# Four feed-forwards of a decoder trunk, each with its own layout of the split weights and direction of the moving rows

## The chip, the cores and the metric

One Trainium2 chip; the program runs on one of its cores. The metric is the device time in microseconds of one execution. PE is the matrix engine (TensorE), with its weight loads shown as PEld; DVE is VectorE, ACT is ScalarE, POOL is GpSimd and SP the engine that issues most transfers.

## The reference, cut to what matters

Two layers, each a half-step feed-forward, a token mixing and a second half-step feed-forward, over 512 tokens of width 1024; the hidden width of a feed-forward is 2816.

```python
def _swiglu(h, wg, wu, wd):
    return (jax.nn.silu(h @ wg) * (h @ wu)) @ wd
...
    for i in range(DEPTH):
        h = _rmsnorm(x, ffn1_norm[i])
        x = x + 0.5 * _swiglu(h, ffn1_w_gate[i], ffn1_w_up[i], ffn1_w_down[i])
        h = _rmsnorm(x, mix_norm[i])
        x = x + _mixing(h, positions, w_in[i], w_out[i], fox_forget_bias[i], lbs[i],
                        hgrn_out_norm[i])
        h = _rmsnorm(x, ffn2_norm[i])
        x = x + 0.5 * _swiglu(h, ffn2_w_gate[i], ffn2_w_up[i], ffn2_w_down[i])
    return _rmsnorm(x, final_norm)
```

The mixing (three token mixers between an input and an output projection) is changed only in where its tiles lie.

## The kernel before, in words

The stream x is kept transposed in on-chip memory: eight tiles x0 to x7 of 128 rows (width) by 512 columns (tokens), in the pool `keep`. Each matrix product with weights is made from float32 values split in two parts of the shorter type float32r: a high part (the value rounded) and a low part (what the rounding left). `split_block` (L182, L184) splits the normalised stream into xh and xl, eight tiles each, also in `keep`. `load_split` (L240 to L245) loads a chunk of weights from memory by a transfer on SP into `raw` (three buffers), writes the high part `wh` by a cast on ACT (L243) and the low part `wl` by a subtraction on DVE (L245), each into a tile of its own with two buffers in the pool `wp`. The two are placed ahead of other work in the order that the scheduler makes (`tc.high_priority(AHEAD)`).

`mm3` (L250 to L252) then issues three matmuls for one slice of 128 by 128 weights: high weights with high rows, high weights with low rows, low weights with high rows. The weights are the stationary operand, loaded before each matmul; the 512 columns of rows are the moving operand, and a PSUM tile of 128 by 512 collects the sum.

`ffn` runs two stages. Gate and up: for each of 22 blocks of the hidden width, a chunk of eight slices of gate weights and one of up weights, 24 matmuls each, into PSUM tiles `gu_ps` (four buffers shared under the name acc). DVE and ACT make silu(gate) x up and split it into hh and hl (L377 to L385), 22 tiles of each in the pool `ffn`. Down: for each of the eight blocks of x, chunks of 8, 7 and 7 slices, 66 matmuls into `d_ps`, then DVE adds half of it to x (L394) and `after` splits and squares the new block (L182 to L194). So a feed-forward has 22 x 2 x 24 = 1056 matmuls of gate and up and 8 x 66 = 528 of down, all of one shape. The kernel has four: the first and the second one of each of two layers. The row norm is summed from squares (`square_block`, L190 to L194, tile sq with two buffers), finished in `norm_finish` (L213 to L231) and applied late, as the row vector rb (two buffers), to the PSUM results. The output projection of the mixing is a shorter run of the same `mm3`, four blocks at a time, which end six matmuls apart.

Where tiles lie follows from the order of the pools and the sizes of their tiles: const (with a spacer `pad` of PAD = 48 words), keep, wp, small, and then ffn or mix in turn. The helper `lines` rounds small tiles up to 64 bytes. All tiles of keep and wp are multiples of 512 bytes, so xh, xl, wh and wl begin at one offset modulo 512 bytes; the tiles of small, between wp and ffn, add up to 128 bytes less than a multiple of 512.

Of the kernel before, what the change touches and what calls it, by code (L numbers as in the profile page):

```python
# [10 lines left out]
F32 = mybir.dt.float32  # L11
# [14 lines left out]
LEVELS = (1, 2, 4, 8, 16, 32, 64)  # L26
AHEAD = 400
CHAIN = 100
PAD = 48


def shape_constants():
# [95 lines left out]
def hybrid_trunk(ctx: ExitStack, tc: tile.TileContext, a, out):  # L128
    nc = tc.nc
    V, S, G, PE = nc.vector, nc.scalar, nc.gpsimd, nc.tensor  # L130

    const = ctx.enter_context(tc.tile_pool(name="const", bufs=1))
    keep = ctx.enter_context(tc.tile_pool(name="keep", bufs=1))
    wp = ctx.enter_context(tc.tile_pool(name="wp", bufs=2))
    small = ctx.enter_context(tc.tile_pool(name="small", bufs=2))
    acc_p = ctx.enter_context(tc.tile_pool(name="acc", bufs=4, space=bass.MemoryType.PSUM))
    gen_p = ctx.enter_context(tc.tile_pool(name="gen", bufs=1, space=bass.MemoryType.PSUM))

# [12 lines left out]
        return gen_p.tile([128, 512], F32, tag=tag, name=name)  # L151


    const.tile([128, PAD], F32, name="pad")
    x = [keep.tile([128, T], F32, name=f"x{k}") for k in range(KB)]
    par = const.tile([128, 64], F32, name="par")
    raws = []
# [17 lines left out]
    def norm_block(k, g, nrm):  # L175

        split_block(k, g)
        square_block(k, nrm)
# [8 lines left out]
    def square_block(k, nrm):  # L187
        if k == 0:
            nrm["ss"] = small.tile([128, T], F32, tag="ss", name="ss", bufs=1)
            S.activation(nrm["ss"], x[k], AF.Square)  # L190
        else:
            sq = small.tile([128, T], F32, tag="sq", name="sq")
            S.activation(sq, x[k], AF.Square)
            V.tensor_tensor(out=nrm["ss"], in0=nrm["ss"], in1=sq, op=ALU.add)  # L194

# [23 lines left out]

    def norm_finish(nrm, copy=True):  # L220
        r = norm_rows(nrm)
        dg = small.tile([128, NB, 128], F32, tag="sq", name="dg")
        for b in range(NB):
            V.tensor_scalar(out=dg[:, b, :], in0=ident, scalar1=r[:, b:b + 1], scalar2=None,
                            op0=ALU.mult)
        ps = gen("pt", "rb_ps")
        PE.matmul(ps, ones, dg.rearrange("p b t -> p (b t)"), start=True, stop=True)
        if not copy:
            return r, ps
        rb = small.tile([128, T], F32, tag="rb", name="rb", bufs=2)  # L230
        S.copy(rb, ps)  # L231
        return r, rb

    def load_split(src, n, cols):

        if raws:
            raw = raws.pop(0)
        else:
            raw = wp.tile([128, n, cols], F32, tag="raw", name="raw", bufs=3)
            nc.sync.dma_start(out=raw, in_=src)  # L240
        with tc.high_priority(AHEAD):
            wh = wp.tile([128, n, cols], R32, tag="wh", name="wh")
            S.copy(wh, raw)  # L243
            wl = wp.tile([128, n, cols], R32, tag="wl", name="wl")
            V.tensor_tensor(out=wl, in0=raw, in1=wh.bitcast(F32), op=ALU.subtract)  # L245
        return wh, wl

    def mm3(ps, lh, ll, rh, rl, first, last):

        PE.matmul(ps, lh, rh, start=first, stop=False)  # L250
        PE.matmul(ps, lh, rl, start=False, stop=False)  # L251
        PE.matmul(ps, ll, rh, start=False, stop=last)  # L252
# [4 lines left out]
    def gvec(key, k):  # L257
        return par[:, gcol[key] + k:gcol[key] + k + 1]
# [101 lines left out]
        lower_bounds()  # L360


    def ffn(l, wg, wu, wd, after, rb, early=None):
        with tc.tile_pool(name="ffn", bufs=1, reuse_waits="tile") as fp:
            hh, hl = [], []
            for j in range(FB):
                if j == 4 and early:
                    early()
                part = []
                for w in (wg, wu):  # L370
                    wh, wl = load_split(w[l, j], KB, 128)
                    ps = acc("gu_ps")
                    for k in range(KB):
                        mm3(ps, wh[:, k, :], wl[:, k, :], xh[k], xl[k], k == 0, k == KB - 1)
                    part.append(ps)
                g = fp.tile([128, T], F32, tag="g", name="g", bufs=2)
                V.tensor_tensor(out=g, in0=part[0], in1=rb, op=ALU.mult)  # L377
                S.activation(g, g, AF.Silu)
                u = fp.tile([128, T], F32, tag="u", name="u", bufs=2)
                V.tensor_tensor(out=u, in0=part[1], in1=rb, op=ALU.mult)  # L380
                V.tensor_tensor(out=u, in0=u, in1=g, op=ALU.mult)  # L381
                h1 = fp.tile([128, T], R32, name=f"hh{j}")
                S.copy(h1, u)  # L383
                h2 = fp.tile([128, T], R32, name=f"hl{j}")
                V.tensor_tensor(out=h2, in0=u, in1=h1.bitcast(F32), op=ALU.subtract)  # L385
                hh.append(h1)
                hl.append(h2)
            for d in range(KB):
                ps = acc("d_ps")
                for j0, j1 in ((0, 8), (8, 15), (15, 22)):  # L390
                    wh, wl = load_split(wd[l, d, :, j0:j1, :], j1 - j0, 128)
                    for j in range(j0, j1):
                        mm3(ps, wh[:, j - j0, :], wl[:, j - j0, :], hh[j], hl[j], j == 0, j == FB - 1)
                V.scalar_tensor_tensor(out=x[d], in0=ps, scalar=0.5, in1=x[d], op0=ALU.mult, op1=ALU.add)  # L394
                after(d)


    def mixing(l, after, r, rb):
# [38 lines left out]
        otl = {kind: [pair(f"ol{kind}", f"ol{kind}", R32)] for kind in "fd"}  # L437
        amat, obl = {}, {}
        at = [lines(mp, [128, 8], tag=f"ad{p}", name=f"ad{p}") for p in range(2)]

        def put_out(kind, b, o, n):

# [215 lines left out]
            return hv  # L658

        ho = [slot(f"ho{b}", (128, 4, 128), f"ho{b}") for b in range(NB)]  # L660
        hss = [lines(mp, [128, NB, 2], tag=f"hss{p}", name=f"hss{p}") for p in range(2)]
        hrs = [None, None]

        def states(p, hv):
            am, ob = amat[p], obl[p]
            for b in range(NB):
                po = gen("lv", "ho_ps")
                for hh in range(2):
                    cross = {
                        (0, 1): ob[:, 2, hh * 256:hh * 256 + 128],  # L670
                        (2, 3): ob[:, 2, hh * 256 + 128:hh * 256 + 256],
                        (0, 2): ob[:, hh, 0:128], (0, 3): ob[:, hh, 128:256],
                        (1, 2): ob[:, hh, 256:384], (1, 3): ob[:, hh, 384:512],
                    }
                    h = 2 * p + hh
                    hs = slice(h * 128, (h + 1) * 128)
                    ps = po[:, hh * 128:(hh + 1) * 128]
                    for j in range(b + 1):
                        lhs = cross[j, b] if j < b else am[:, hh, b * 128:(b + 1) * 128]
                        PE.matmul(ps, lhs, hv[j // 2][:, j % 2, hs], start=j == 0, stop=j == b)  # L680
                    V.scalar_tensor_tensor(out=ho[b][:, h, :], in0=hv[b // 2][:, b % 2, hs],
                                           scalar=at[p][:, hh * NB + b:hh * NB + b + 1], in1=ps,
                                           op0=ALU.mult, op1=ALU.add)
                    sq = mp.tile([128, 128], F32, tag="hsq", name="hsq", bufs=1)
                    S.activation(sq, ho[b][:, h, :], AF.Square, accum_out=hss[p][:, b, hh:hh + 1])
                yield
            ss = hss[p]
            V.tensor_scalar(out=ss, in0=ss, scalar1=1.0 / 128, scalar2=EPS, op0=ALU.mult, op1=ALU.add)
            hrs[p] = rsqrt(ss.rearrange("p b h -> p (b h)"), [128, 8], f"hr{p}")
# [51 lines left out]
    for l in range(L):  # L741
# [8 lines left out]
        nrm = {}  # L750
        if l + 1 < L:
            ffn(l, a["ffn2_w_gate"], a["ffn2_w_up"], a["ffn2_w_down"],
                lambda d: norm_block(d, gvec(("ffn1_norm", l + 1), d), nrm), rb)
            r, rb = norm_finish(nrm)
        else:
            def last(d):
                square_block(d, nrm)
                if d == KB - 2:
                    warm = lines(small, [128, 1], tag="warm", name="warm")
                    S.activation(warm, nrm["ss"][:, 0:1], AF.Sqrt)  # L760

            ffn(l, a["ffn2_w_gate"], a["ffn2_w_up"], a["ffn2_w_down"], last, rb)
            _, rb = norm_finish(nrm, copy=False)
            for d in range(KB):
                V.scalar_tensor_tensor(out=x[d], in0=x[d], scalar=gvec("final", d), in1=rb,
                                       op0=ALU.mult, op1=ALU.mult)
                (nc.scalar if d % 2 else nc.sync).dma_start(out=out[d * 128:(d + 1) * 128, :], in_=x[d])
# [17 lines left out]
```

## Time and profile before

| | |
|---|---|
| median of 3 runs | 2109.16 us (2108.77 to 2109.34) |
| the profiled execution's own time | 2108.85 us |
| its span, first to last instruction | 2107.1 us |
| PE busy | 2080.3 us, 99% of the span |
| DVE, ACT busy | 993.5 us (47%), 691.6 us (33%) |
| mean granted TensorE clock | 0.997 of full speed |

Matmuls are pipelined: a record of a 512-column matmul is some 390 ns long and overlaps the next one, so what a matmul costs is the distance from its start to the next start, and the busy share of PE alone does not tell it.

### The profile page before, as it was taken

How to read it: one execution, taken by the hardware profiler on the slowest of the kernel's cores; microseconds unless marked ns; L12 is line 12 of the kernel's file. 1: busy time of each engine (PE TensorE's matmuls, PEld its weight loads, DVE VectorE, ACT ScalarE, POOL GpSimd, SP SyncE). 2: the span in 40 equal slices, each digit the busy share in tenths (PEclk: the TensorE clock that was granted, in tenths of full speed). 3: DMA queues.
4: the chain of work that ended last, by engine and by line, in shares of the span. 5: the costliest groups of instructions: out<-in, count | busy, mean ns of one | idle time of the engine just before them, and what ended most of it. 6: DMA issues, size and time to landing. Idle time of an engine off the chain costs nothing.

```text
span 2107.1 us, 23700 instructions
## 1 busy us (share of the span) xinstructions
PE 2080.3 (99%) x9622; PEld 1688.9 (80%) x9622; DVE 993.5 (47%) x1590; ACT 691.6 (33%) x1005; POOL 13.0 (1%) x18
## 2 busy tenths in 40 slices
PE   8999999999999999999999999999999999999997
PEld 6888888888777888888888888888887778888885
DVE  7444433556364544443344443336554554444323
ACT  5323222333353423222233322232344443323221
POOL 0000000000000000000000000000000000000000
PEclk9999999999999999999999999999999999999998
DMA  5322333211122222233332223332211122222332
GB/s 166 100 91 99 95 93 94 94 60 51 50 69 67 97 92 99 100 94 92 95 98 93 100 96 91 99 100 70 65 57 51 56 85 90 100 98 92 95 96 69
DMA packets 54373, 184.35 MB, mean 87 GB/s; under 512 B 6888, under 2 KB 7016, under 8 KB 54264
## 3 DMA queue, kind: packets, MB, share of 16 engines
q1 hardware_dynamic: 53656, 181.73, 27.1%
q8 instruction: 75, 1.23, 0.2%
q10 hardware_dynamic: 576, 1.05, 0.1%
q14 instruction: 34, 0.28, 0.0%
q0 software_dynamic: 32, 0.07, 0.0%
HBM read 180.69 MB, written 2.10 MB: 87 GB/s over the span
## 4 chain that ended last, share of the span: by engine, by line
PE 97%; DVE 2%; ACT 1%; DMA 0%; issue 0%; SPq 0%; DVEq 0%
PE gu_ps L252 15%; PE gu_ps L251 15%; PE gu_ps L250 15%; PE d_ps L252 8%; PE d_ps L250 8%; PE d_ps L251 8%; PE lv_ps L501 2%; PE sc_ps L552 2%; PE po L571 2%; PE o_ps L250 1%; PE o_ps L251 1%; PE o_ps L252 1%; PE ho_ps L680 1%; PE pt_ps L564 1%; PE v_ps L425 1%; PE v_ps L426 1%
## 5 line engine op out<-in xcount | busy, mean ns | idle before, releaser
L243 ACT CAST wh<-raw 128x1024 fp32r<-128x1024 f32 (+2 forms) x350 | 357.6, 1022 | 1112.7 <-issue 417.4
L245 DVE TENSOR_TENSOR wl<-raw,wh 128x1024 fp32r<-128x1024 f32 (+2 forms) x350 | 415.5, 1187 | 321.5 <-ACT wh L243 319.4
L250 PE MATMUL gu_ps<-xh,wh 128*128 128x512 f32 x1408 | 548.8, 390 | 7.5 <-ACT wh L243 7.5
L252 PE MATMUL gu_ps<-xh,wl 128*128 128x512 f32 x1408 | 550.4, 391 | 0.0
L251 PE MATMUL gu_ps<-xl,wh 128*128 128x512 f32 x1408 | 548.3, 390 | 0.0
L250 PEld LDWEIGHTS gu_ps<-xh,wh 128*128 128x128 f32 x1408 | 264.9, 188 | 63.6 <-ACT wh L243 7.5
L252 PEld LDWEIGHTS gu_ps<-xh,wl 128*128 128x128 f32 x1408 | 264.8, 188 | 56.1 <-issue 1.0
L251 PEld LDWEIGHTS gu_ps<-xl,wh 128*128 128x128 f32 x1408 | 264.8, 188 | 55.4 <-DVE xl L184 0.2
L252 PE MATMUL d_ps<-hh,wl 128*128 128x512 f32 x704 | 278.1, 395 | 0.0
L250 PE MATMUL d_ps<-hh,wh 128*128 128x512 f32 x704 | 278.1, 395 | 0.0
L251 PE MATMUL d_ps<-hl,wh 128*128 128x512 f32 x704 | 278.1, 395 | 0.0
L380 DVE TENSOR_TENSOR u<-gu_ps,rb 128x512 f32<-128x512 f32 x88 | 60.8, 691 | 269.2 <-PE gu_ps L252 269.0
L252 PEld LDWEIGHTS d_ps<-hh,wl 128*128 128x128 f32 x704 | 132.1, 188 | 32.2
L251 PEld LDWEIGHTS d_ps<-hl,wh 128*128 128x128 f32 x704 | 132.1, 188 | 32.1
L250 PEld LDWEIGHTS d_ps<-hh,wh 128*128 128x128 f32 x704 | 132.1, 188 | 32.1
L377 DVE TENSOR_TENSOR g<-gu_ps,rb 128x512 f32<-128x512 f32 x88 | 60.8, 691 | 178.7 <-PE gu_ps L252 176.6
L383 ACT CAST hh<-u 128x512 fp32r<-128x512 f32 x88 | 54.8, 623 | 61.2 <-DVE u L381 61.2
L394 DVE SCALAR_TENSOR_TENSOR x<-d_ps,x 128x512 f32<-128x512 f32 x32 | 22.1, 692 | 95.3 <-PE d_ps L252 95.3
L381 DVE TENSOR_TENSOR u<-u,g 128x512 f32<-128x512 f32 x88 | 60.9, 692 | 8.4
L501 PEld LDWEIGHTS lv_ps<-hQ,hk 128*128 128x128 f32 x448 | 55.8, 191 | 8.7 <-issue 5.9
L385 DVE TENSOR_TENSOR hl<-u,hh 128x512 fp32r<-128x512 f32 x88 | 60.3, 686 | 4.1 <-ACT hh L383 4.1
L571 PEld LDWEIGHTS po<-vv,pt 128*128 128x128 f32 x320 | 42.2, 190 | 19.7 <-DVE pt L569 7.8
(236 smaller groups left out, 2104.8 us busy)
## 6 DMA issues: line engine op xcount, KB each, us to landing
raw<-in_ffn_w_gate SPq DMA_DIRECT2D x88, 512.0 KB, 3.5
raw<-in_ffn_w_up SPq DMA_DIRECT2D x88, 512.0 KB, 3.5
raw<-in_w_in SPq DMA_DIRECT2D x58, 512.0 KB, 3.5
raw<-in_ffn_w_down SPq DMA_DIRECT2D x64, 448.0 KB, 3.3
raw<-in_ffn_w_down SPq DMA_DIRECT2D x32, 512.0 KB, 3.5
raw<-in_w_out_dh SPq DMA_DIRECT2D x16, 384.0 KB, 2.9
x<-in_x SPq DMA_DIRECT2D x8, 256.0 KB, 6.3
raw<-in_w_out_f SPq DMA_DIRECT2D x4, 512.0 KB, 3.6
```

What stands on the lines that cost most here:

```text
L243: S.copy(wh, raw)
L245: V.tensor_tensor(out=wl, in0=raw, in1=wh.bitcast(F32), op=ALU.subtract)
L250: PE.matmul(ps, lh, rh, start=first, stop=False)
L251: PE.matmul(ps, lh, rl, start=False, stop=False)
L252: PE.matmul(ps, ll, rh, start=False, stop=last)
L377: V.tensor_tensor(out=g, in0=part[0], in1=rb, op=ALU.mult)
L380: V.tensor_tensor(out=u, in0=part[1], in1=rb, op=ALU.mult)
L381: V.tensor_tensor(out=u, in0=u, in1=g, op=ALU.mult)
L383: S.copy(h1, u)
L385: V.tensor_tensor(out=h2, in0=u, in1=h1.bitcast(F32), op=ALU.subtract)
L501: PE.matmul(ps[:, e:e + 64], K[:, hh, s], Q[:, hh, s].rearrange("p (n two c) -> p n two c", two=2, c=c)[:, :, 1, :], start=True, stop=True)
L571: PE.matmul(po[:, h * HD:(h + 1) * HD], pt[:, j * 128:(j + 1) * 128], val[:, j, h * HD:(h + 1) * HD], start=j == 0, stop=j == b)
```

## The change

Each feed-forward gets a layout for the two parts of its weights and a direction for its moving rows. High and low part now share one tile `ww`. In layer 0 (mode "apart") each slice's 128 high words and 128 low words follow one another, each with a gap of 16 words. In layer 1 (mode "mixed") high and low words alternate, so that each part lies at every second word, with 16 words of gap after a slice's 256. The mixing keeps all high slices ahead of all low ones. In the second feed-forward of each layer (`turned`) the moving rows are read, and the PSUM columns written, from the last to the first. The pools are put in another order with other spacers; sq, rb and dg have one buffer; two small tiles of the mixing move.

```diff
-PAD = 48
+PAD = 96
...
-    const = ctx.enter_context(tc.tile_pool(name="const", bufs=1))
+    align = ctx.enter_context(tc.tile_pool(name="align", bufs=1))
     keep = ctx.enter_context(tc.tile_pool(name="keep", bufs=1))
     wp = ctx.enter_context(tc.tile_pool(name="wp", bufs=2))
+    const = ctx.enter_context(tc.tile_pool(name="const", bufs=1))
     small = ctx.enter_context(tc.tile_pool(name="small", bufs=2))
+    fill = ctx.enter_context(tc.tile_pool(name="fill", bufs=1))
...
-    const.tile([128, PAD], F32, name="pad")
+    align.tile([128, 32], F32, name="pad0")
+    fill.tile([128, PAD], F32, name="pad1")
...
-            sq = small.tile([128, T], F32, tag="sq", name="sq")
+            sq = small.tile([128, T], F32, tag="sq", name="sq", bufs=1)
...
-        dg = small.tile([128, NB, 128], F32, tag="sq", name="dg")
+        dg = small.tile([128, NB, 128], F32, tag="sq", name="dg", bufs=1)
...
-        rb = small.tile([128, T], F32, tag="rb", name="rb", bufs=2)
+        rb = small.tile([128, T], F32, tag="rb", name="rb", bufs=1)
...
-    def load_split(src, n, cols):
+    def load_split(src, n, cols, mode=None):
...
-            wh = wp.tile([128, n, cols], R32, tag="wh", name="wh")
+            ww = wp.tile([128, n * (2 * cols + (32 if mode == "apart" else 16 if mode else 0))], R32, tag="ww", name="ww")
+            if mode == "mixed":
+                ww = ww.rearrange("p (n c) -> p n c", n=n)[:, :, 0:2 * cols].rearrange("p n (c two) -> p n two c", two=2)
+            elif mode == "apart":
+                ww = ww.rearrange("p (n two c) -> p n two c", n=n, two=2)[:, :, :, 0:cols]
+            else:
+                ww = ww.rearrange("p (two n c) -> p n two c", n=n, two=2)
+            wh, wl = ww[:, :, 0, :], ww[:, :, 1, :]
             S.copy(wh, raw)
-            wl = wp.tile([128, n, cols], R32, tag="wl", name="wl")
             V.tensor_tensor(out=wl, in0=raw, in1=wh.bitcast(F32), op=ALU.subtract)
         return wh, wl
 
-    def mm3(ps, lh, ll, rh, rl, first, last):
-
+    def mm3(ps, lh, ll, rh, rl, first, last, turned=False):
+
+        if turned:
+            ps, rh, rl = ps[:, ::-1], rh[:, ::-1], rl[:, ::-1]
...
-    def ffn(l, wg, wu, wd, after, rb, early=None):
+    def ffn(l, wg, wu, wd, after, rb, early=None, turned=False):
+        mode = "mixed" if l else "apart"
...
-                    wh, wl = load_split(w[l, j], KB, 128)
+                    wh, wl = load_split(w[l, j], KB, 128, mode)
...
-                    wh, wl = load_split(wd[l, d, :, j0:j1, :], j1 - j0, 128)
+                    wh, wl = load_split(wd[l, d, :, j0:j1, :], j1 - j0, 128, mode)
...
-                    sq = mp.tile([128, 128], F32, tag="hsq", name="hsq", bufs=1)
+                    sq = small.tile([128, 128], F32, tag="sq", name="hsq", bufs=1)
...
-            ffn(l, a["ffn2_w_gate"], a["ffn2_w_up"], a["ffn2_w_down"], last, rb)
+            ffn(l, a["ffn2_w_gate"], a["ffn2_w_up"], a["ffn2_w_down"], last, rb, turned=True)
```

## Rows read from the trace of the kernel before

**Rows 1.** The page's head and its part 1, busy time by engine.
```profile
span 2107.1 us, 23700 instructions
...
PE 2080.3 (99%) x9622; PEld 1688.9 (80%) x9622; DVE 993.5 (47%) x1590; ACT 691.6 (33%) x1005; POOL 13.0 (1%) x18
```

**Rows 2.** The chain of waits that ended last, its shares by line.
```profile
PE gu_ps L252 15%; PE gu_ps L251 15%; PE gu_ps L250 15%; PE d_ps L252 8%; PE d_ps L250 8%; PE d_ps L251 8%; PE lv_ps L501 2%; PE sc_ps L552 2%; PE po L571 2%; PE o_ps L250 1%; PE o_ps L251 1%; PE o_ps L252 1%; PE ho_ps L680 1%; PE pt_ps L564 1%; PE v_ps L425 1%; PE v_ps L426 1%
```

**Rows 3.** Costliest groups: shape, count, busy us, mean ns, idle before, its releaser.
```profile
L243 ACT CAST wh<-raw 128x1024 fp32r<-128x1024 f32 (+2 forms) x350 | 357.6, 1022 | 1112.7 <-issue 417.4
L245 DVE TENSOR_TENSOR wl<-raw,wh 128x1024 fp32r<-128x1024 f32 (+2 forms) x350 | 415.5, 1187 | 321.5 <-ACT wh L243 319.4
L250 PE MATMUL gu_ps<-xh,wh 128*128 128x512 f32 x1408 | 548.8, 390 | 7.5 <-ACT wh L243 7.5
...
L252 PEld LDWEIGHTS gu_ps<-xh,wl 128*128 128x128 f32 x1408 | 264.8, 188 | 56.1 <-issue 1.0
...
L252 PE MATMUL d_ps<-hh,wl 128*128 128x512 f32 x704 | 278.1, 395 | 0.0
```

**Rows 4.** Windows: stretch, us, busy us (count) of each engine, PEclk, DMA.
```profile
30.00:250.00 220.00, 220.00 (x972) 182.21 (x972) 114.05 (x195) 71.49 (x91) 0.00 (x0) 1.00 0.30 96
252.00:374.00 122.00, 122.00 (x525) 98.14 (x524) 42.29 (x47) 32.58 (x39) 0.95 (x1) 1.00 0.32 93
```

**Rows 5.** Timeline of PE: start us, length us, instruction; the ends of down.
```profile
251.72 0.40 PE L250 MATMUL d_ps<-hh,wh 128*128 128x512 f32 x1
...
374.69 0.39 PE L252 MATMUL d_ps<-hh,wl 128*128 128x512 f32 x1
```

**Rows 6.** Timeline of PE inside gate and up, and inside down.
```profile
80.36 0.39 PE L250 MATMUL gu_ps<-xh,wh 128*128 128x512 f32 x1
80.59 0.39 PE L251 MATMUL gu_ps<-xl,wh 128*128 128x512 f32 x1
...
300.02 0.39 PE L250 MATMUL d_ps<-hh,wh 128*128 128x512 f32 x1
300.25 0.40 PE L251 MATMUL d_ps<-hl,wh 128*128 128x512 f32 x1
300.49 0.39 PE L252 MATMUL d_ps<-hh,wl 128*128 128x512 f32 x1
300.71 0.40 PE L250 MATMUL d_ps<-hh,wh 128*128 128x512 f32 x1
```

**Rows 7.** Timeline of PE after a break, an FK product of the mixing.
```profile
611.86 0.40 PE L250 MATMUL fk_ps<-xh,wh 128*128 128x512 f32 x1
612.10 0.39 PE L251 MATMUL fk_ps<-xl,wh 128*128 128x512 f32 x1
612.32 0.39 PE L252 MATMUL fk_ps<-xh,wl 128*128 128x512 f32 x1
...
613.71 0.39 PE L252 MATMUL fk_ps<-xh,wl 128*128 128x512 f32 x1
613.94 0.39 PE L250 MATMUL fk_ps<-xh,wh 128*128 128x512 f32 x1
```

**Rows 8.** Timeline of PE at the kernel's start; four matmuls lie between these two.
```profile
9.81 0.63 PE L251 MATMUL gu_ps<-xl,wh 128*128 128x512 f32 x1
...
11.94 0.63 PE L250 MATMUL gu_ps<-xh,wh 128*128 128x512 f32 x1
```

**Rows 9.** The chain in order of time, one level of the decay product.
```profile
434.95 1.73 PE lv_ps L501 x16
```

**Rows 10.** Groups of DVE and ACT, the whole span.
```profile
L510 DVE TENSOR_TENSOR hQ<-hQ,hf 128x512 f32<-128x512 f32 x28 | 19.4, 692 | 0.0
...
L194 DVE TENSOR_TENSOR ss<-ss,sq 128x512 f32<-128x512 f32 x49 | 33.7, 687 | 1.1 <-ACT sq L193 0.7
L193 ACT ACTIVATE sq<-x 128x512 f32<-128x512 f32 x49 | 30.1, 619 | 10.7 <-DVE x L394 9.8 <-DVE ss L194 0.8
```

**Rows 11.** Waits: who waited for whom, us in all, times, longest us.
```profile
ACT wh L243 <- PE d_ps L251: 273.7, 72, 4.1
```

More of the change, by code (lines that the diff above doesn't have):

```diff
@@ L370, in ffn @@
                 for w in (wg, wu):
-                    wh, wl = load_split(w[l, j], KB, 128)
+                    wh, wl = load_split(w[l, j], KB, 128, mode)
                     ps = acc("gu_ps")
                     for k in range(KB):
-                        mm3(ps, wh[:, k, :], wl[:, k, :], xh[k], xl[k], k == 0, k == KB - 1)
+                        mm3(ps, wh[:, k, :], wl[:, k, :], xh[k], xl[k], k == 0, k == KB - 1, turned)
                     part.append(ps)
@@ L390, in ffn @@
                 for j0, j1 in ((0, 8), (8, 15), (15, 22)):
-                    wh, wl = load_split(wd[l, d, :, j0:j1, :], j1 - j0, 128)
+                    wh, wl = load_split(wd[l, d, :, j0:j1, :], j1 - j0, 128, mode)
                     for j in range(j0, j1):
-                        mm3(ps, wh[:, j - j0, :], wl[:, j - j0, :], hh[j], hl[j], j == 0, j == FB - 1)
+                        mm3(ps, wh[:, j - j0, :], wl[:, j - j0, :], hh[j], hl[j], j == 0, j == FB - 1, turned)
                 V.scalar_tensor_tensor(out=x[d], in0=ps, scalar=0.5, in1=x[d], op0=ALU.mult, op1=ALU.add)
@@ L439, in mixing @@
         at = [lines(mp, [128, 8], tag=f"ad{p}", name=f"ad{p}") for p in range(2)]
+        hss = [lines(mp, [128, NB, 2], tag=f"hss{p}", name=f"hss{p}") for p in range(2)]
         def put_out(kind, b, o, n):
@@ L660, in mixing @@
         ho = [slot(f"ho{b}", (128, 4, 128), f"ho{b}") for b in range(NB)]
-        hss = [lines(mp, [128, NB, 2], tag=f"hss{p}", name=f"hss{p}") for p in range(2)]
         hrs = [None, None]
@@ L752, in hybrid_trunk @@
             ffn(l, a["ffn2_w_gate"], a["ffn2_w_up"], a["ffn2_w_down"],
-                lambda d: norm_block(d, gvec(("ffn1_norm", l + 1), d), nrm), rb)
+                lambda d: norm_block(d, gvec(("ffn1_norm", l + 1), d), nrm), rb, turned=True)
             r, rb = norm_finish(nrm)
```

## The prediction

> **What bounds the kernel.** I read the page from the top. The span is 2107.1 us and PE is busy in 99% of it; DVE at 47% and ACT at 33% are not near [rows 1]. The profiled execution took 2108.85 us, so 1.75 us lie around the span, and the median of the runs, 2109.16, is 0.3 us above it; I sum against 2108.9 and give the result against the median. The chain of waits is PE for 97%; the three product lines of the feed-forwards make 3 x 15% (gate and up) and 3 x 8% (down), 69% of the span, some 1454 us [rows 2]. So the time is the number of feed-forward matmuls times the distance between their starts. The numbers are 4224 (gate and up) and 2112 (down) in the groups [rows 3]: for each of the four feed-forwards 1056 and 528. The change keeps every one of them; only the distance can move.
>
> The distance comes from the windows [rows 4]. 972 matmuls in 220 us; a record is 390 ns long, so about 1.7 of them hang over the edges: 220/970.3 = **226.7 ns** for gate and up. 122/(525 - 1.7) = 233.1 for down; there the first and the last matmul of a stage start at 251.72 and 374.69, 527 distances, **233.3 ns** [rows 5], which I use. The granted clock is 1.00 in all. [...]
>
> [...] In the timeline gate/up ticks evenly, 0.22 to 0.23, while down changes between 0.22 and 0.24 from one matmul to the next [rows 6]; operation, shape and clock are the same. What differs is where the operands lie: by the sizes of the tiles in the code, weights and xh/xl start at the same offset modulo 512 bytes, while hh/hl start 128 bytes off. After a break, in one FK product of the mixing, which reads xh like gate/up, the first distances are uneven (0.24, 0.22, 0.23), and ten matmuls later it is back at 0.23 [rows 7]: something locks in. [...] The load has time: 188 ns a record, and about 40 ns of idle before each [rows 3].
>
> [...]
>
> **The change, part by part.**
> Apart (layer 0): slices of high and low part stand next to each other, each with 64 bytes of gap, so the place relative to the moving row changes with every k. Ends: it keeps the locked 226.7, or runs unlocked as in down, 233.3. I take the middle, 230: 1056 x 3.3 = +3.5 us for each of the two feed-forwards; down is unlocked already and stays. Together **+7.0**.
> Mixed (layer 1): the weights lie every second word, so the load walks 1024 bytes in place of 512. How long a load streams is seen in the decay product, whose matmuls have 64 columns and are bound by it: 16 records in 1.73 us, 108 ns each [rows 9]. [...] Taking the middle between none and the 13.3 of gate/up, 220, for both stages: 1056 x 6.7 + 528 x 13.3 = 7.1 + 7.0 = **-14.1** in the forward one. No row shows a weight load with a stride; a load at half its rate would take 216 ns and still fit under 226.7.
> Turned (the second feed-forward of each layer): moving rows and PSUM columns go backwards. No row shows a backward walk. For apart I price it at 0 (the readers still pass each other). For mixed the two now walk against each other; I take half of the gain: **-7.0**. Whether rows or PSUM go slower backwards is a rival below.
> The split writes: ACT's cast and DVE's subtraction now write (mixed) every second word. DVE's product on half of Q at stride two, in the first level, costs the same as on others (the group's mean is 692 ns for 512 elements, like the unstrided ones) [rows 10]; ACT has no such row. Cover: 24 matmuls take 5.4 us, the split 1.0 + 1.2 [rows 3], so twice the price would hide. Cost 0; without cover some 350 x 1.1.
> One tile for both parts: the cast's buffer is released by the last L252 in place of L251, 0.23 us later. Behind the cast on ACT stand the silu and hh, behind these DVE's hl, whose readers come only in down. In down, the casts now wait 273.7 us in all for L251, 72 waits of 4.1 us at most, which are slack [rows 11]. 0. At the head the first L250 might wait for the low part too, 1.2 us; PE's first groups end before the row norm is there. 0, upper end 1.3.
> One buffer for the squares: ACT's square waits for DVE's add of the one before. In the end of the output projection, four blocks come 6 matmuls (1.4 us) apart against 0.62 + 0.69 for square and add [rows 10]: at the limit; +0.5 for each layer, **+1**. At the head the same, under PE's first products. rb with one buffer: its readers end long before the next copy. 0.
> The output projection's rows move too: 384 matmuls between 226.7 and 233: within 2.6 us, taken as 0. DMAs and queues are unchanged: the same loads in the same order on SP.
>
> Sum: 7.0 - 14.1 - 7.0 + 1 = -13.1; 2108.9 - 13 = 2095.8, against the median **2096**.
>
> **Rivals.**
> 1. The lock is lost (slower, 0.20): what makes 226.7 cheap is equal offsets, and both layouts take these away. For it: down, the long stage with unequal offsets, stands at 233. [...] It decides if gate/up of layer 1 stands over 226.7. 4224 x 6.7 = +28: 2137.
> 2. The surplus is paid for each stretch of memory that the weight load touches (0.10): mixed touches twice as many. [...] Mixed surplus doubled: 2112 x 13.3 + 1056 x 20 = +49: 2158.
> 3. Walking backwards is slow in itself (0.10): moving rows or PSUM writes at half rate, 213.3 more for each of 3168 turned matmuls: +676, 2785. Nothing in the trace shows such a walk. [...]
> 4. The readers do not meet (0.12), the surplus belongs to the matmul; the layout does nothing, 2109 within 4.
> 5. All four feed-forwards drop to half of the gate/up surplus (0.06): -6.7 x 4224 - 13.3 x 2112 = -56: 2053.
>
> **How the numbers follow.** The forecast's own case, mixed wins more than apart loses, has 0.42; its own range is from 2075 (mixed without surplus both ways: 1056 x 13.3 + 528 x 20 = 24.6 each, with apart at +14) to 2105. With rivals 1, 2 and 4 the range is 2045 to 2175; it leaves out rival 3, and the ends of the others. A measurement here tells about 0.2%, 4.2 us, from no change. Faster: 0.42 + 0.06 = 0.48. Same: 0.12. Slower: 0.20 + 0.10 + 0.10 = 0.40.
>
> **What the profile of the changed kernel would show.** The four feed-forwards are four readings, each in two stages. Right: layer 0 between 226.7 and 233.3 in gate and up, layer 1 at or below 220 forward, and weight loads that still fit. Wrong: layer 1 at or over 226.7 (rivals 1, 2); turned ones far above the forward ones of their layer (3); all as before (4). If the casts' waits on PE turn into PE's waits on the casts, the split was not covered.

## The result, and the profile after

The changed kernel takes 2124.97 us (median of 4 runs, 2124.01 to 2125.41) against 2109.15: ratio 1.0074 with a 95% interval of 1.0059 to 1.0089, **15.8 us slower**. The forecast was 2096, faster. The page of the changed kernel answers to [rows 1] and [rows 3]:

```profile
span 2122.8 us, 23694 instructions
...
PE 2097.5 (99%) x9622; PEld 1710.3 (81%) x9622; DVE 993.5 (47%) x1590; ACT 700.9 (33%) x1005; POOL 13.1 (1%) x18
...
L254 ACT CAST ww<-raw 128x1024 fp32r<-128x1024 f32 (+2 forms) x350 | 370.1, 1057 | 1142.2 <-issue 438.1
L255 DVE TENSOR_TENSOR ww<-raw,ww 128x1024 fp32r<-128x1024 f32 (+2 forms) x350 | 415.4, 1187 | 346.0 <-ACT ww L254 345.7
L262 PE MATMUL gu_ps<-xh,ww 128*128 128x512 f32 x1408 | 556.5, 396 | 7.6 <-ACT ww L254 7.6
```

The split costs nearly what it did (DVE 1187 ns as before, ACT 1057 for 1022), the count of matmuls is the same, and the waits of the casts on PE, now on L264 in place of L251, are still slack: 250.6 us in down against 273.7 in [rows 11]. The weight loads still fit: at every second word, in gate and up of layer 1, a record takes 193 to 195 ns, for 188 in [rows 3].

```profile
ACT ww L254 <- PE d_ps L264: 250.6, 66, 3.9
...
L263 PEld LDWEIGHTS gu_ps<-xl,ww 128*128 128x128 f32 x303 | 59.1, 195 | 11.8
```

So the time is in the distance from one matmul's start to the next, its tick in what follows. Windows of PE alone, by stage, in the order apart forward, apart turned, mixed forward, mixed turned; gate and up first, then down (stretch, us, busy us and count, clock, DMA), to be read as [rows 4]:

```profile
40.00:240.00 200.00, 200.00 (x871) 1.00 0.30 95
260.00:370.00 110.00, 110.00 (x478) 1.00 0.32 94
710.00:920.00 210.00, 210.00 (x901) 1.00 0.29 93
940.00:1050.00 110.00, 110.00 (x474) 1.00 0.32 93
1080.00:1290.00 210.00, 210.00 (x908) 1.00 0.29 95
1310.00:1420.00 110.00, 110.00 (x477) 1.00 0.32 94
1760.00:1970.00 210.00, 210.00 (x902) 1.00 0.29 93
1990.00:2100.00 110.00, 110.00 (x473) 1.00 0.29 83
```

Each tick is the stretch over the count less 1.7, good to some 0.4 ns:

| ns a matmul | gate and up | down |
|---|---|---|
| before, all four | 226.7 | 233.3 |
| apart forward | 230.1 | 230.9 |
| apart turned | 233.5 | 232.9 |
| mixed forward | 231.7 | 231.4 |
| mixed turned | 233.3 | 233.4 |

Against before, gate and up of the four lose 1056 x (3.4 + 6.8 + 5.0 + 6.6) = 23.0 us and down wins about 528 x (2.4 + 0.4 + 1.9 - 0.1) = 2.4. That is 20.6; the measured 15.8 leaves some 5 us won elsewhere. The starts of the matmuls in the traces show where: the 384 of the output projection take 97.7 us before and 92.7 now. Experiment 5 comes back to it.

The prediction and the expectations count a surplus from 213.3 ns a matmul, which no run shows. The lowest ticks that the runs show are 215.7 to 215.9 (experiments 3, 4 and 6); over these, before has 10.8 ns in gate and up and 17.5 in down, 4224 x 10.8 + 2112 x 17.5 = 83 us in all.

### The profile page after: what moved, and what is told of

The parts are those of the page before. It is cut to its first block, busy times and chain, and to the rows that moved or that the text cites. A ratio compares the mean times of both kernels' runs of the same rounds, so it can differ in the third digit from the quotient of the medians.

```text
span 2122.8 us, 23694 instructions
## 1 busy us (share of the span) xinstructions
PE 2097.5 (99%) x9622; PEld 1710.3 (81%) x9622; DVE 993.5 (47%) x1590; ACT 700.9 (33%) x1005; POOL 13.1 (1%) x18
## 4 chain that ended last, share of the span: by engine, by line
PE 97%; DVE 2%; ACT 1%; DMA 0%; issue 0%; SPq 0%; DVEq 0%; ACTq 0%
PE gu_ps L264 15%; PE gu_ps L262 15%; PE gu_ps L263 15%; PE d_ps L264 8%; PE d_ps L262 8%; PE d_ps L263 8%; PE lv_ps L515 2%; PE sc_ps L566 2%; PE po L585 2%; PE o_ps L263 1%; PE o_ps L262 1%; PE o_ps L264 1%; PE ho_ps L693 1%; PE pt_ps L578 1%; PE v_ps L438 1%; PE v_ps L439 1%
## 5 line engine op out<-in xcount | busy, mean ns | idle before, releaser
L254 ACT CAST ww<-raw 128x1024 fp32r<-128x1024 f32 (+2 forms) x350 | 370.1, 1057 | 1142.2 <-issue 438.1
L255 DVE TENSOR_TENSOR ww<-raw,ww 128x1024 fp32r<-128x1024 f32 (+2 forms) x350 | 415.4, 1187 | 346.0 <-ACT ww L254 345.7
L262 PE MATMUL gu_ps<-xh,ww 128*128 128x512 f32 x1408 | 556.5, 396 | 7.6 <-ACT ww L254 7.6
L263 PE MATMUL gu_ps<-xl,ww 128*128 128x512 f32 x1408 | 557.8, 396 | 0.0
L264 PE MATMUL gu_ps<-xh,ww 128*128 128x512 f32 x1408 | 557.7, 396 | 0.0
L262 PEld LDWEIGHTS gu_ps<-xh,ww 128*128 128x128 f32 x1408 | 269.8, 192 | 65.0 <-ACT ww L254 7.6
L263 PEld LDWEIGHTS gu_ps<-xl,ww 128*128 128x128 f32 x1408 | 269.8, 192 | 59.2 <-issue 1.0
L264 PEld LDWEIGHTS gu_ps<-xh,ww 128*128 128x128 f32 x1408 | 269.2, 191 | 58.6 <-DVE ww L255 0.8
L264 PE MATMUL d_ps<-hh,ww 128*128 128x512 f32 x704 | 278.5, 396 | 0.0
L263 PE MATMUL d_ps<-hl,ww 128*128 128x512 f32 x704 | 278.1, 395 | 0.0
L262 PE MATMUL d_ps<-hh,ww 128*128 128x512 f32 x704 | 277.9, 395 | 0.0
L263 PEld LDWEIGHTS d_ps<-hl,ww 128*128 128x128 f32 x704 | 134.7, 191 | 29.0
L262 PEld LDWEIGHTS d_ps<-hh,ww 128*128 128x128 f32 x704 | 134.7, 191 | 28.9
L264 PEld LDWEIGHTS d_ps<-hh,ww 128*128 128x128 f32 x704 | 134.4, 191 | 28.8
```

## The experiments

The four feed-forwards of a run are four readings, given in order; a word has 4 bytes. All kernels stand on the changed one unless said otherwise, with `FEED` naming (layout, turned) of each feed-forward, by layer and place in it; None is the plain layout, all high slices ahead of all low ones, and a number shifts the plain weights by so many words. A time without a ratio is that of a single run; there the ticks are what is read.

**1. Plain layout, forward; then turned.**

```diff
-        mode = "mixed" if l else "apart"
+    FEED = {(0, 1): (None, False), (0, 2): (None, False), (1, 1): (None, False), (1, 2): (None, False)}
...
+        mode, turned = FEED[l, which]
```

> The changed kernel's pools and spacers, but all four feed-forwards with the plain layout (all high slices, then all low ones) and forward rows. Weights begin 256 bytes off hh/hl and at the same place modulo 256 as xh/xl. Offset theory: a matmul's distance locks at 226.7 ns when weights and moving row begin a multiple of 256 bytes apart, so gate/up 226.7 and down 226.7 in all four (down was 233.3 before), time 2109 - 2112 x 6.6 ns = 2095 us. Rival (the spacers do nothing, layout and direction alone cost): down stays at 233.3, time 2109.

Measured: 2090.43 us against 2109.09, ratio 0.9912 (0.9895 to 0.9928). The second row is down: 100/(442 - 1.7) = 227.1, one edge of a count from the 226.7 of gate and up above it.

```profile
40.00:240.00 200.00, 200.00 (x884) 1.00 0.30 97
260.00:360.00 100.00, 100.00 (x442) 1.00 0.33 97
```

```diff
+    FEED = {(0, 1): (None, False), (0, 2): (None, True), (1, 1): (None, False), (1, 2): (None, True)}
```

> As plain, with the second feed-forward of each layer turned (rows read and PSUM written from the last to the first). Direction theory: a backward walk costs in itself and ticks at 233.3 with any layout, so gate/up and down of the second feed-forwards at 233.3, time about 2095 + 3168 x 6.6 ns = 2116 us. Rival (direction costs only with the new layouts, whose offsets were lost): they lock at 226.7 as the forward ones, time 2095.

Measured: 2112.9 us. The second feed-forward's two windows give 233.3 and 233.5, the first stays at 226.7. The second's two:

```profile
700.00:910.00 210.00, 210.00 (x902) 1.00 0.29 93
940.00:1040.00 100.00, 100.00 (x430) 1.00 0.32 95
```

So offset and direction each cost by themselves, without the new layouts.

**2. Which place, and which layout.** First the start of the weights is shifted, in words.

```diff
+                off = mode or 0
+                ww = ww[:, off:off + n * 2 * cols].rearrange("p (two n c) -> p n two c", n=n, two=2)
...
+    FEED = {(0, 1): (16, False), (0, 2): (32, False), (1, 1): (8, False), (1, 2): (4, False)}
```

> As plain, all forward, but the weights' tile begins 64 bytes later in the first feed-forward, 128 later in the second, 32 in the third, 16 in the fourth. Offset theory: each loses the lock; 128 bytes gives 233.3 in both stages (as down before), 64 bytes between 230 and 234, and 32 and 16 bytes either still 226.7 (if what counts is a block of 64 bytes or more) or 230 to 234 (if it is finer). Rival (what counted was not the offset): 226.7 in all.

Measured: 2132.0 us; 233.3, 232.5, 233.3, 233.5. None stays at 226.7, not even at 16 bytes. The first and the fourth:

```profile
40.00:240.00 200.00, 200.00 (x859) 1.00 0.29 94
...
1760.00:1970.00 210.00, 210.00 (x901) 1.00 0.29 93
```

Two more runs differ in the shifts alone (48, 24, 1, 60 words; then 63, 62, 56, 52).

> As the run with shifted weight tiles, with shifts of 192, 96, 4 and 240 bytes. Offset theory with a period of 256 bytes: none of them locks at 226.7; 192 and 240 stand, by symmetry, like 64 and 16 bytes (233.3 each), 96 and 4 bytes between 230 and 234. If some offset lets the readers miss each other, a cell below 226.7 shows it; I expect none.

Measured: 2114.9 us; 229.0, 234.3, 232.5 and, at 240 bytes, 226.7. The symmetry that I expected isn't there:

```profile
40.00:240.00 200.00, 200.00 (x875) 1.00 0.30 95
700.00:910.00 210.00, 210.00 (x898) 1.00 0.29 95
1070.00:1280.00 210.00, 210.00 (x905) 1.00 0.29 93
1750.00:1960.00 210.00, 210.00 (x928) 1.00 0.31 96
```

> As the run with shifted weight tiles, with 252, 248, 224 and 208 bytes, that is 4, 8, 32 and 48 bytes short of a full period. The shift of 240 (16 short) locked at 226.7, while 16 bytes over did not. If the lock has a width below the period's end: 252, 248 and perhaps 224 lock at 226.7, 208 stands near 229 as 192 does. If only a multiple of 16 bytes locks: 252 and 248 stand over 230, 224 locks. A cell below 226.7 would be a new place to gain; I expect none.

Measured: 2131.9 us; 233 in all four, 4 bytes short of 256 too:

```profile
40.00:240.00 200.00, 200.00 (x858) 1.00 0.29 93
```

In all three runs down, whose weights by the sizes of the tiles lie 256 bytes further from their rows, ticks as its gate and up do, within the error. So the differences tried repeat after 256 bytes, and modulo 256 only 0 and 240 tick at 226.7. The difference doesn't settle every tick: at 128 bytes it is 232.5 here, and 233.3 in down of the kernel before; what the rest hangs on is not shown.

The shifts also give the tick of apart forward. There high slices lie 0 and 128 bytes off in turn, low ones 64 and 192, and two matmuls of three take a high slice: from 226.7, 232.5, 233.3 and 229.0 this estimates 230.1, and gate and up measured 230.1, down 230.9.

Next, the layouts without gaps.

```diff
+            elif mode == "mixed0":
+                ww = ww[:, 0:n * 2 * cols].rearrange("p (n c two) -> p n two c", n=n, two=2)
+            elif mode == "apart0":
+                ww = ww[:, 0:n * 2 * cols].rearrange("p (n two c) -> p n two c", n=n, two=2)
...
+    FEED = {(0, 1): ('apart0', False), (0, 2): ('apart0', True), (1, 1): ('mixed0', False), (1, 2): ('mixed0', True)}
```

> Layouts without their gaps: high and low slices next to each other in layer 0, high and low words alternating in layer 1, every slice a multiple of 256 bytes from the moving row; the second feed-forward of each layer turned. Offset theory: the first feed-forward locks at 226.7 in both stages, since layout itself costs nothing; mixed forward at 226.7 too or, if the forecast's equal-rates reading holds, below 220; turned ones at 233.3. Rival (layout costs in itself): 230 to 232 in the first and third, as in the changed kernel.

Measured: 2128.0 us; gate and up of the four:

```profile
40.00:240.00 200.00, 200.00 (x884) 1.00 0.30 97
700.00:910.00 210.00, 210.00 (x902) 1.00 0.29 93
1070.00:1280.00 210.00, 210.00 (x901) 1.00 0.29 95
1750.00:1960.00 210.00, 210.00 (x889) 1.00 0.28 92
```

226.7, 233.3, 233.5, 236.7. Apart costs nothing once its gaps are gone; mixed costs 6.7 even so, and a further 3 backward. The equal-rates reading, on which the forecast stood, was my guess that weights at every second word and a moving row are walked at one rate; no row showed it, and the gain that it was to bring isn't here: mixed forward is no step towards 220. Its weight loads take 193 ns a record for 188, so the load did not become slow in itself.

**3. Is it the weight load at all?** Narrower weights, then a reader that stands still.

```diff
...
-        PE.matmul(ps, lh, rl, start=False, stop=False)
...
+        PE.matmul(ps[0:v], lh[:, 0:v], rl, start=False, stop=False)
...
```

> As plain, but all matmuls of a group except its first and last use only the first 112 (first feed-forward), 96, 80, 64 (fourth) columns of the weight slice, so the weight load is shorter while the 512 moving rows stay; part of each product is left out. If the surplus of 13.3 ns over 213.3 is what the weight load takes from the moving rows, it shrinks with the load: 213.3 + 13.3 x 112/128 = 225.0, then 223.3, 221.7, 220.0. If it belongs to the matmul: 226.7 in all four.

Measured: 2116.3 us; 229.8, 230.2, 232.7, 229.9: no shrinking with the load. The fourth, with half of the columns:

```profile
1750.00:1960.00 210.00, 210.00 (x915) 1.00 0.30 95
```

With 8, 32, 66 and 120 columns:

> As plain, with all matmuls of a group but its first and last on the first 8 (first feed-forward), 32, 66 and 120 (fourth) columns of the slice; part of each product is left out. If the surplus is made by the weight load at all, 8 columns, a load of 32 bytes, must bring the distance near to the 215.8 that a moving row standing still has; 32 columns in between. If it is made by the moving rows alone: 226 to 233 in all four.

Measured: 2115.5 us; 226.7, 231.2, 232.2, 232.7. The 8 columns, their window and a row of their loads:

```profile
40.00:240.00 200.00, 200.00 (x884) 1.00 0.31 96
...
L269 PEld LDWEIGHTS gu_ps<-xl,ww 128*8 128x8 f32 x294 | 25.8, 88 | 37.1
```

A load of 32 bytes, 88 ns a record in place of 188, leaves the tick at 226.7, so it isn't the load's length. Of the lengths tried, only 8 and 128 tick at 226.7; the others cost more, as other places do.

```diff
+        if "w" in v:
+            lh, ll = [t[:, 0:1].to_broadcast([128, 128]) for t in (lh, ll)]
+        if "r" in v:
+            rh, rl = [t[:, 0:1].to_broadcast([128, 512]) for t in (rh, rl)]
```

> As plain, but in the first feed-forward the weight load reads one word of each slice 128 times, in the second the moving row is one word read 512 times, in the third both, in the fourth none; the products are then not those of the reference. If the surplus comes from two readers passing over the same places, a reader that stands still changes it: nearer to 213.3 in the first three (or up, if it stands in the other's way). If it belongs to the matmul or to the load's length: 226.7 in all.

Measured: 2063.4 us. Weights standing still: 200/865.3 = 231.1. A row standing still: 200/926.3 = 215.9, and in down 100/463.3 = 215.8, with full weight loads beside it. With both standing still it is 216.4, and 215.8 in down, and the untouched fourth has 226.7.

```profile
40.00:240.00 200.00, 200.00 (x867) 1.00 0.30 95
...
700.00:900.00 200.00, 200.00 (x928) 1.00 0.32 100
920.00:1020.00 100.00, 100.00 (x465) 1.00 0.35 102
```

So some 10.8 of the 226.7 ns go with the walk of the moving row. Every matmul of these kernels has a weight load of its own (9622 of each on the page), so whether a straight walk would cost 226.7 with no load beside it is not shown.

**4. Which walk.**

```diff
+        if "r" in v:
+            rh, rl = rh[:, ::-1], rl[:, ::-1]
+        if "p" in v:
+            ps = ps[:, ::-1]
```

> As plain, but in the first feed-forward only the moving rows are read backwards, in the second only the PSUM columns are written backwards, in the third both, in the fourth none; where one alone is backwards the tokens of that product come out in reverse order. If the backward read meets the weight load in another way: rows only 233.3, PSUM only 226.7, both 233.3, none 226.7. If the backward write is what costs: 226.7, 233.3, 233.3, 226.7.

Measured: 2110.7 us; 233.3, 226.7, 233.3, 226.7: the backward read costs, the backward write costs nothing.

```profile
40.00:240.00 200.00, 200.00 (x859) 1.00 0.29 93
...
710.00:920.00 210.00, 210.00 (x928) 1.00 0.30 97
```

```diff
+        if v == "high":
+            ll = lh
+        elif v == "low":
+            lh = ll
+        elif v:
+            rh, rl = [t[:, 0:v].unsqueeze(1).to_broadcast([128, 512 // v, v]) for t in (rh, rl)]
+            ps = ps.rearrange("p (n c) -> p n c", c=v)
```

> All forward. First feed-forward: the layout of alternating words without gaps, all three matmuls on the high words (offset 0, every second word); second: all three on the low words (offset 4 bytes); third: plain weights, the moving row's first 128 words read four times; fourth: its first 16 words read 32 times; the products are not those of the reference. If every second word costs in itself: 233 in the first; if only the 4 bytes of the low words did: 226.7 in the first, over 230 in the second. [...]

Measured: 2136.6 us; 233.3, 233.3, 226.7, 241.9. The first and the fourth:

```profile
40.00:240.00 200.00, 200.00 (x859) 1.00 0.30 94
...
1750.00:1960.00 210.00, 210.00 (x870) 1.00 0.28 90
```

Weights at every second word cost in themselves, without the 4 bytes. A short walk isn't a cheap one: 16 words over and over are the dearest of these four.

```diff
+        if v < 0:
+            rh, rl = [t.rearrange("p (a c) -> p a c", c=-v)[:, ::-1, :] for t in (rh, rl)]
+        else:
+            rh, rl = [t.rearrange("p (a c) -> p c a", a=v) for t in (rh, rl)]
+        ps = ps.rearrange("p (a c) -> p a c", c=rh.shape[2])
```

> As plain, with the moving row's words in another order, written to PSUM in the order they come, so the products are not those of the reference: blocks of 128 words from last to first (first feed-forward), blocks of 16 words from last to first (second), word i and i+256 in turn (third), words i, i+128, i+256, i+384 in turn (fourth). If what a backward read costs is the order of the 64-byte blocks: 226.7, 233.3; if it is the order within them: 226.7, 226.7. [...]

Measured: 2173.1 us; gate and up of the four:

```profile
40.00:240.00 200.00, 200.00 (x884) 1.00 0.30 96
700.00:910.00 210.00, 210.00 (x902) 1.00 0.29 93
1070.00:1270.00 200.00, 200.00 (x929) 1.00 0.31 101
1720.00:1980.00 260.00, 260.00 (x919) 1.00 0.24 77
```

226.7 for blocks of 128 words from last to first, 233.3 for blocks of 16: turning blocks of 64 bytes, each read forward, has the whole price of a backward read, turning blocks of 512 bytes has none. Sizes between, and a turn inside the blocks alone, were not tried. And the third, word i and i+256 in turn, runs at 200/927.2 = **215.7**; the fourth, with four places in turn, at 283.4.

**5. The offset alone.** The kernel before, plus one spacer:

```diff
+    fill = ctx.enter_context(tc.tile_pool(name="fill", bufs=1))
+    fill.tile([128, 32], F32, name="pad1")
```

> The kernel before with one edit: a spacer of 128 bytes between small and ffn, so that hh/hl, and the mixing's tiles, begin at the weights' place modulo 256 bytes. Offset theory: down locks at 226.7 in all four (2112 x 6.67 = 14.1 us less) and the output projection at 227 (384 x 5 = 1.9 us less): 2109.1 - 16 = 2093 us, and what plain has beyond that is of its other edits. Rival (the pools' new order or the absolute place matters): less than half of that.

Measured: 2093.58 us against 2108.65, ratio 0.9928 (0.9912 to 0.9945); its down is at 100/(443 - 1.7) = 226.6:

```profile
260.00:360.00 100.00, 100.00 (x443) 1.00 0.34 98
```

Plain is 3 us better: that much is won by its other edits (pools, single buffers, one tile, the moved tiles of the mixing), which I didn't separate. By the starts in the traces it is won in the output projection, which takes 97.7 us before, 96.4 with the spacer, and 92.7 in plain as in the changed kernel: these are the 5 us left over in the result, 1.3 by the spacer and 3.7 by the other edits. A wait of PE there for ohf, a tile that ACT writes, 1.5 us in all, stands in the lists of waits of the first two and not in those of the others.

**6. A version that beats both.** Rows stored with even tokens first, read in turn, so that PSUM has its own order:

```diff
+            hi, lo, xx = halves2(hi), halves2(lo), evens(xx)
...
+            rh, rl = [t.rearrange("p (two i) -> p i two", two=2) for t in (rh, rl)]
+            ps = ps.rearrange("p (i two) -> p i two", two=2)
...
-                S.copy(h1, u)
+                S.copy(halves2(h1), evens(u))
```

> The plain kernel, with the feed-forwards' moving rows stored with the even tokens in the first half of the tile and the odd ones in the second, and read back word 0, 256, 1, 257 and so on, so that PSUM holds the tokens in their own order and nothing is left out. If the walk's order alone makes the surplus, as the run on orders has it: 215.8 ns in both stages of all four, 6336 x 10.84 = 68.7 us below plain, 2090.4 - 68.7 = 2022 us, ACT and DVE writing from every second word at the price they have now. Rival (with real rows, or against the real weights, the readers meet all the same): 226.7 or more, 2090. A second rival: the strided reads of ACT and DVE cost enough to hold PE up: distance 215.8, but waits of PE on hh, hl or xh.

Measured: 2024.61 us against 2109.58, ratio **0.9598** (0.9582 to 0.9614). Gate and up 200/926.3 = 215.9, down 215.8; ACT's cast of hh and DVE's hl, which now read every second word, take 875 and 835 ns, for 623 and 686 before, and PE doesn't wait for them. The cast of before stands last:

```profile
span 2023.1 us, 23692 instructions
...
L413 ACT CAST hh<-u 128x512 fp32r<-128x512 f32 x88 | 77.0, 875 | 40.7 <-DVE u L411 40.7
L415 DVE TENSOR_TENSOR hl<-u,hh 128x512 fp32r<-128x512 f32 x88 | 73.4, 835 | 1.9 <-ACT hh L413 1.9
...
L383 ACT CAST hh<-u 128x512 fp32r<-128x512 f32 x88 | 54.8, 623 | 61.2 <-DVE u L381 61.2
```

The two windows of the first feed-forward:

```profile
40.00:240.00 200.00, 199.99 (x928) 1.00 0.32 100
250.00:350.00 100.00, 100.00 (x465) 1.00 0.35 103
```

Against plain that is 65.8 us, for 68.7 expected: the ticks are the expected ones, and the pauses of PE in gate and up grew by some 2.5 us, 0.9 of them waits for xh.

```diff
+    FEED = {(0, 1): (16, False), (0, 2): (32, False), (1, 1): (8, False), (1, 2): ('mixed0', False)}
```

> As woven, with the weights' tile 64 bytes later in the first feed-forward, 128 in the second, 32 in the third, and every-second-word weights without gaps in the fourth. If the surplus is gone for good in the woven order, the place and the stride of the weights no longer matter: 215.8 in all. If only the aligned case is free: 222 or more in the first three, over that in the fourth.

Measured: 2024.8 us; 215.8 in all four. The third and the fourth, the fourth with every second word:

```profile
1030.00:1230.00 200.00, 200.00 (x929) 1.00 0.32 102
...
1680.00:1880.00 200.00, 200.00 (x929) 1.00 0.32 101
```

In the woven order the three shifts and the stride of the weights cost nothing, where a straight row had 232 to 234 with each of them. A woven row in the turned direction was not tried.

## Why the prediction was wrong, point by point

The forecast's parts against the ticks, gate and up with down: apart forward +3.5, measured +2.3; apart turned +3.5, measured +7.0; mixed forward -14.1, measured +4.3; mixed turned -7.0, measured +7.0; the rest +1, measured about -5, which leaves the 15.8. The time lies far outside the forecast's own range, 2075 to 2105; the wide range holds it through rival 1 and not through the forecast's reason.

No run shows the 213.3 ns from which the forecast's 13.3 and 20, its ranges and the prices of rivals 2, 3 and 5 are counted, nor at which rates, or where to each other, a weight load and a moving row are walked. The runs showed 215.7 to 215.9 as the lowest ticks, of a row that stands still or is read from its two halves in turn, and 231.4 to 236.8 wherever the weights lay at every second word beside a row walked forward or backward.

- **The bound** was right: PE's distances set the time. The split writes, the later release and the casts' waits stayed covered. Outside the feed-forwards the terms, +1 for the squares and 0 for the output projection, were mis-sized: the projection got 5.0 us shorter, and PE's wait for the sum of the squares is 2.4 us for 2.3.
- **The reading of the surplus** is the step that failed, and with it the forecast. My reading, the next matmul's weight load in the way of the moving rows, had the right witness (the distance depends on addresses, 226.7 and 233.3 before) and the wrong seat: 8 columns of load leave 226.7, a standing or woven row takes it to 215.8 beside full loads. So 10.8 of the 226.7 ns hang on the order in which the row is walked; what the weights' place, stride or length adds, up to 7.6 ns in a forward row, was seen on top of a straight walk only. I read a dependence on two addresses as a meeting of two walks, and never asked what a row costs that walks otherwise.
- **Mixed**, -14.1 forward: measured +5.3 in gate and up and -1.0 in down, +4.3. The pace of the load was read rightly: its records take 88 ns for 8 columns and 188 for 128, from which I estimate 0.83 ns a column, 107 for 128, against 108 in the prediction; at every second word they take only 5 to 7 ns more. But the hoped-for gain was not there: aligned and at every second word it is 233.
- **Turned**, priced at 0 on top of apart's +3.5, and at -7.0 for mixed: +7 in both, nearly all in gate and up. The backward read has a price of its own, 6.6 ns on aligned plain rows, as much as the gap between before's two ticks; down was at that price already.
- **Apart**, +3.5 forward: +3.6 in gate and up, -1.3 in down. The size of gate and up was right and so was the reason, the lost offset: without gaps it is 226.7. That the middle of the two ends fits so well is luck; the shifts of experiment 2 are what gives 230.1. Down's gain was not foreseen.
- **Rival 1**, the lock is lost, happened: layer 1 stood over 226.7, which was its condition. Its price, +28, was too high by some 12 us: the two forward cells stop at 230 to 232, down there is won, and the output projection gave 5 us back. Its reason holds for apart alone; mixed and turned cost when aligned too.
- Rival 2, the surplus goes by the stretch that the load touches, has the same condition, but mixed forward measured 231.7 in gate and up, not the 240.0 of 13.3 more, and 231.4 in down, below before. Rivals 4 and 5 fell, since the ticks moved, and up.
- Rival 3 had the right operation, backward reading, which costs 6.6 ns, a thirtieth of its price; the backward writing that it names beside it cost nothing, with 226.7.

With straight rows the place of the weights alone moved the tick from 226.7 to 234.3; with woven rows it was 215.8 at every place tried.

Why a straight walk costs 226.7 and a woven one 215.8, and why four places in turn cost 283, is not shown by any run.

## What to carry to other kernels

Measure the distance from start to start of matmuls stage by stage, against the lowest that any order of the same operands shows; 10.8 and 17.5 ns there were some 83 us here, behind a busy share of 99%, and the woven order's ticks won them. Before arranging two operands around each other, take one of them out (stand it still, shrink it) to see whose the cost is. For rows of float32r as long as these, try the woven order, and failing that, put weights and rows at one place modulo 256 bytes, both walking forward and neither with a stride.

## What was not expected of the hardware

- A moving row of 512 float32r words read in turn from its two halves: 215.8 ns; read straight: 226.7 at best; from four quarters: 283; 16 words over and over: 241.9.
- The straight read ticks at 226.7 with weights 0, 240 or 256 bytes off; 4 or 16 bytes over, and 4 or 8 short of 256, give 232 to 234.
- Writing PSUM backward cost nothing; a weight load at every second word took 193 to 195 ns for 188.
